# A hybrid attention and RWKV layer, its instructions ordered by the framework's timeline model

## Chip, core and metric

The kernel runs on one core of a Trainium2 chip. The metric is the device time of one execution in microseconds (us). Three runs of the kernel before gave a median of 2612.89 us (2607.87 to 2619.28).

## The reference, cut to what matters

One layer is computed for 1024 prompt tokens and for 32 decode tokens that have 256 earlier ones in a cache. All sizes are fp32; the model width is 2048, there are 8 attention heads of width 128 (two maps of 64 each) and 16 RWKV heads of 64.

```python
xn = rms_norm(x, norm_g)
proj = xn @ w_in                      # 2048 x 8320: q, k, v, gate, RWKV r/k/v, LoRA, gate
q = rope(rms_norm(q, q_norm_g), pos); k = rope(rms_norm(k, k_norm_g), pos)
o = diff_attention(q, k, v)           # (softmax of map 0 - lam * softmax of map 1) @ v, chunk mask
att_out = rms_norm(o, subln_g) * (1 - lam_init) * silu(g_att)
# RWKV-7, per token: S = S * w_t + (S a_t) b_t^T + v_t k_t^T ; y_t = S r_t
y = group_norm(wkv_scan(r, decay, k, v, -kk, kk * a, wkv0)) * lnx_g + lnx_b + bonus
rw_out = y * silu(g_rw)
out = x + concat(att_out, rw_out) @ w_out
```

## The kernel before

The tokens are worked in two halves. Half A is 512 prompt tokens and the 32 decode tokens, 544 columns in two chunks of 288 and 256; half B is the other 512 prompt tokens in one chunk. In each half there are eight units. Unit u stands for one attention head and one pair of RWKV heads and runs eight projections (q, k, v, attention gate, RWKV r, k, v and gate). A projection (`proj`) has 16 blocks of the contraction, and each fp32 product is made of three in a rounded format (`xh` by `wh`, `xl` by `wh`, `xh` by `wl`), so it is 48 matmuls for each chunk, into a PSUM bank named `pj` of which there are three. All matmuls are recorded at L92, transposes on TensorE at L97. Behind the units come 16 output projections for each half.

Weights arrive by GpSimd's DMA queue in 256 KB pieces (`wr`, two buffers; L231), are rounded by ScalarE (`wh`, L224), and the remainder is taken by VectorE (`wl`, L225; three buffers each). A finished bank is read by VectorE, which multiplies it with the row scale (`normed`, L351), and this frees the bank.

Everything else is put between the projections. RWKV of a unit is done for two sub-blocks of four or five chunks of 64 tokens: a preparation (`rw_down`: products of `AR` and `BK` in the bank `Y`, masked into `MM` at L765; a solver of 31 steps on VectorE, L784 and L786, between two trips through DRAM), then a chain (`rw_chain`) with one round per chunk of tokens. A round has three steps on TensorE in the bank `ch`, each with a handoff to other engines: `ch<-Sw,AR` (then L893 on ScalarE and `xs`, L896 on VectorE), `ch<-xs,TT` (then `UV`, L902 on ScalarE and L903 on VectorE), `ch<-UV,MM` (then the new state `Sw`, L908, and the output `Yt`, L916, on VectorE). The next round starts from the new `Sw`. Attention has the steps of q and k (norm through the bank `am`, rotation at L437 to L440, split at L446 and L462, in buffers of the tag `t`, four), the turning of v (`vT`, also a `t`; transposes in `am`), and for each of four query blocks the scores in the bank `sc`, the maximum over them (L556), exponentials, transposes of `E` in `sc`, and the product with `Vt` in `am`. PSUM is full: three banks `pj`, one each of `ch`, `am` and `Y`, two for `sc`.

The order is set twice. When the kernel is written out, its own planner does it: six streams (chain, preparation, q and k, post, attention, decay) are generators that yield a latency from the table `LAT`; between the matmuls of a projection `pump()` lets each stream go on whose due time has been passed by a clock that counts the matmuls written so far:

```python
                if k < KT - 1:
                    if k % 4 == 3 or (k % 2 == 1 and n == 512):
                        pump()
                    else:
                        chs.run()
```

Then the framework's scheduler takes the written program. It lets instructions pass engine by engine; among those that its model of time has as ready, the one with the highest priority goes, which is the one written first, or one written under `tc.high_priority()`, as the weights are. On the chip each engine runs its instructions strictly in the resulting order.

## Time and profile before

| | |
|---|---|
| median of three runs | 2612.89 us |
| the profiled execution: its time | 2613.46 us |
| its span | 2611.7 us |
| TensorE (PE) busy | 2549.7 us, 98% |
| VectorE (DVE) busy | 1892.0 us, 72% |
| ScalarE (ACT) busy | 1349.6 us, 52% |
| GpSimd (POOL) busy | 415.1 us, 16% |
| mean granted clock of TensorE | 0.995 |

The profiled execution is one run of the kernel; its times are those of the rows below. A share of busy time is a mean over the whole span. PEld is TensorE's loading of weights, which runs beside its matmuls. An fp32 matmul that isn't in the rounded format stands as two records in the trace. A matmul's duration runs to the modelled end of its pipeline, so two that follow each other overlap in the timeline. The granted clock is given as a share of 2.4 GHz; 0.50 is 1.2 GHz.

### The profile page before, as it was taken

The numbers are of one execution on the slowest core, as the hardware profiler recorded it, in microseconds if no ns is written. First come the engines' busy times: TensorE is split into PE (matmuls) and PEld (weight loads), VectorE is DVE, ScalarE is ACT, GpSimd is POOL, SyncE is SP. The second block draws the span as 40 slices with busy tenths as digits, with TensorE's granted clock in tenths as the row PEclk, the third lists the DMA queues.
The fourth block names the chain that finished last, engine by engine and source line by source line (L and its number), as shares of the span: only waits on it lengthen the run. The fifth ranks groups of instructions, "written<-read, shape, count | busy, mean of one in ns | idle before, by whom it ended". The sixth has DMA issues, their size and how long they took to land. (4 is left out here: it accounts for less than half of the span.)

```text
span 2611.7 us, 49090 instructions
## 1 busy us (share of the span) xinstructions
PE 2549.7 (98%) x17128; PEld 2220.1 (85%) x17128; DVE 1892.0 (72%) x5768; ACT 1349.6 (52%) x3138; POOL 415.1 (16%) x949
## 2 busy tenths in 40 slices
PE   7999999999999999999999999999999999999999
PEld 7999999999898999877777777777777778999887
DVE  7576877777777787788787887788878888753432
ACT  6455555555555655565555555555555556332321
POOL 3211111111111111111111111111111111111000
PEclk9999999999999999999999999999999999999999
DMA  4433332324242524353332323232324244544443
GB/s 156 119 102 94 93 103 84 110 82 115 75 122 80 170 72 122 98 153 100 98 98 87 103 83 106 85 111 81 114 81 115 77 132 118 176 148 140 137 142 108
DMA packets 198665, 286.74 MB, mean 110 GB/s; under 512 B 102097, under 2 KB 115921, under 8 KB 198417
## 3 DMA queue, kind: packets, MB, share of 16 engines
q0 software_dynamic: 51088, 169.12, 21.8%
q1 hardware_dynamic: 147328, 114.47, 15.5%
q8 instruction: 136, 2.23, 0.4%
q14 instruction: 113, 0.92, 0.1%
HBM read 228.11 MB, written 37.51 MB: 102 GB/s over the span
## 5 line engine op out<-in xcount | busy, mean ns | idle before, releaser
L92 PE MATMUL pj<-xh,wh 128*128 128x256 f32 (+2 forms) x3888 | 1294.2, 333 | 7.7 <-ACT xh L248 6.7
L92 PE MATMUL pj<-xl,wh 128*128 128x256 f32 (+2 forms) x3888 | 1274.7, 328 | 5.0 <-DVE xl L249 5.0
L92 PE MATMUL pj<-xh,wl 128*128 128x256 f32 (+2 forms) x3888 | 1272.5, 327 | 1.1 <-DVE wl L225 1.1
L92 PEld LDWEIGHTS pj<-xh,wh 128*128 128x128 f32 x3888 | 735.7, 189 | 61.2 <-ACT xh L248 7.0
L92 PEld LDWEIGHTS pj<-xl,wh 128*128 128x128 f32 x3888 | 736.2, 189 | 52.5 <-DVE xl L249 8.8
L92 PEld LDWEIGHTS pj<-xh,wl 128*128 128x128 f32 x3888 | 735.4, 189 | 52.4 <-DVE wl L225 2.1
L224 ACT CAST wh<-wr 128x512 fp32r<-128x512 f32 x584 | 360.6, 618 | 471.8 <-PE pj L92 420.1
L225 DVE TENSOR_TENSOR wl<-wr,wh 128x512 fp32r<-128x512 f32 x584 | 401.2, 688 | 193.5 <-ACT wh L224 162.9
L231 POOL DMA_DIRECT2D wr<-w_in x517 | 278.3, 538 | 1639.8 <-DVE wl L225 492.2
L786 DVE TENSOR_TENSOR ts<-tm,ts 64x54 f32<-64x54 f32 (+35 forms) x992 | 198.2, 200 | 15.1
L784 DVE TENSOR_TENSOR tm<-ts,ms 64x54 f32<-64x54 f32 (+35 forms) x992 | 197.7, 199 | 14.5 <-DMA ts<-tinit 0.2
L92 PEld LDWEIGHTS ch<-UV,MM 64*64 64x64 f32 (+2 forms) x1632 | 111.5, 145 | 38.1 <-DVE UV L903 9.2
L92 PE MATMUL ch<-UV,MM 64*64 64x64 f32 (+2 forms) x1632 | 128.9, 231 | 8.0 <-DVE UV L846 5.1
L899 ACT ACTIVATE SP<-Sw,PL 64x64 f32<-64x64 f32 x256 | 88.3, 345 | 91.2 <-DVE Sw L908 78.1
L225 DVE TENSOR_TENSOR wl<-MM,wh 128x512 fp32r<-128x512 f32 x64 | 44.0, 689 | 89.1 <-ACT wh L224 89.1
L224 ACT CAST wh<-MM 128x512 fp32r<-128x512 f32 x64 | 39.6, 620 | 128.9 <-PE pj L92 123.3
L896 DVE TENSOR_TENSOR xs<-ch,MM 64x64 f32<-64x64 f32 x272 | 58.6, 216 | 50.2 <-ACT RS L893 45.7
L908 DVE SCALAR_TENSOR_TENSOR Sw<-ch,PL,SP 64x64 f32<-64x64 f32 x256 | 70.7, 276 | 23.2 <-PE ch L92 16.7
L92 PE MATMUL am<-Vt,E 128*128 128x128 f32 (+1 forms) x592 | 84.7, 280 | 1.8 <-ACT wh L224 1.1
L92 PE MATMUL Y<-AR,BK 64*128 64x128 f32 x544 | 84.8, 290 | 0.7 <-DVE MM L765 0.6
L92 PEld LDWEIGHTS Y<-AR,BK 64*128 64x128 f32 x544 | 67.5, 188 | 19.8 <-issue 9.1
L92 PEld LDWEIGHTS am<-Vt,E 128*128 128x128 f32 (+1 forms) x592 | 73.5, 189 | 8.7 <-issue 2.6
(303 smaller groups left out, 3127.9 us busy)
## 6 DMA issues: line engine op xcount, KB each, us to landing
wr<-w_in POOLq DMA_DIRECT2D x517, 256.0 KB, 3.2
wr<-w_out POOLq DMA_DIRECT2D x64, 256.0 KB, 3.6
MM<-w_out POOLq DMA_DIRECT2D x32, 512.0 KB, 4.0
t<-xB SPq DMA_DIRECT2D x32, 256.0 KB
ms<-dm SPq DMA_DIRECT2D x96, 64.0 KB
t<-t SPq DMA_DIRECT2D x64, 68.0 KB
t<-mixd SPq DMA_DIRECT2D x16, 272.0 KB
t<-xA SPq DMA_DIRECT2D x16, 272.0 KB
```

The lines of the kernel that those rows point to most:

```text
L92: PE.matmul(out, lhsT, rhs, start=start, stop=stop)
L224: S.copy(wh, raw)
L225: V.tensor_tensor(wl, raw, wh.bitcast(F32), op=ALU.subtract)
L231: q.dma_start(raw, wsrc[:, g * 512:(g + 1) * 512].rearrange("p (k f) -> p k f", k=4))
L784: V.tensor_tensor(tm, ts_[:, 0:qn, s:s + 1].to_broadcast([R * nb, qn, m]), ms[:, s:s + 1, s + 1:32].to_broadcast([R * nb, qn, m]), op=ALU. ...
L786: V.tensor_tensor(ts_[:, 0:qn, s + 1:32], tm, ts_[:, 0:qn, s + 1:32], op=ALU.add)
L896: V.tensor_tensor(xs[64 * h:64 * h + 64], ch[low, 64 * h:64 * h + 64], MM[low, c, h, 0:64], op=ALU.add)
L899: S.activation(SP[:, h, :], S_[hr, h, :], AF.Copy, scale=PL[hr, 0, gc:gc + 1])
L908: V.scalar_tensor_tensor(S_[hr, h, :], ch[low, 192 + 64 * h:256 + 64 * h], PL[low, h, gc:gc + 1], SP[:, h, :], ALU.mult, ALU.add)
```

## The change

One argument is added where the framework's context is opened. What the kernel writes is unchanged, its planner and the table too. The scheduler, which orders the written program when it is built, now decides what is ready by another model of time, one that keeps timelines of engines, queues and DMAs.

```diff
-    with tile.TileContext(nc) as tc:
+    with tile.TileContext(nc, schedule_with_timeline_sim=True) as tc:
         build(tc, I, O)
```

No instruction is added, removed or changed by it; each engine has the same ones in another order. Numbers behind a name tell tiles of one tag apart, and xN stands for N alike in a row.

**Unit 3 (half A), TensorE.** Before, one round of the chain (bank `ch_1246`), from its first to its second step; `pj_1240` is the second bank of the RWKV r projection of unit 3:

```order
L92 MATMUL ch_1246_6781<-Sw_1245_6770,AR_1022_5589 128x128
L92 MATMUL pj_1240_6759<-xh0_19_104,wh_1242_6762 128x256
L92 MATMUL pj_1240_6759<-xl0_20_105,wh_1242_6762 128x256
L92 MATMUL pj_1240_6759<-xh0_19_104,wl_1243_6763 128x256
L92 MATMUL pj_1240_6759<-xh1_22_111,wh_1242_6762 128x256
L92 MATMUL pj_1240_6759<-xl1_23_112,wh_1242_6762 128x256
L92 MATMUL pj_1240_6759<-xh1_22_111,wl_1243_6763 128x256
L92 MATMUL pj_1240_6759<-xh2_25_118,wh_1242_6762 128x256
L92 MATMUL pj_1240_6759<-xl2_26_119,wh_1242_6762 128x256
L92 MATMUL pj_1240_6759<-xh2_25_118,wl_1243_6763 128x256
L92 MATMUL pj_1240_6759<-xh3_29_127,wh_1242_6762 128x256
L92 MATMUL ch_1246_6781<-xs_1248_6785,TT_9_79 128x64
```

Now the same round, to its third step; `Y_1143` and `Y_1157` belong to the preparation of the next sub-block, `am_1144` to the norm of q, `am_1195` to the norm of k of unit 3:

```order
L92 MATMUL ch_1246_6781<-Sw_1245_6770,AR_1022_5589 128x128
L92 MATMUL Y_1143_6231<-AR_1119_6070,BK_1109_6013 128x128 x4
L92 MATMUL am_1144_6237<-p3_1124_6100,blkr_85_252 128x272
L92 MATMUL am_1144_6237<-p3_1125_6101,blkr_85_252 128x272
L92 MATMUL ch_1246_6781<-xs_1248_6785,TT_9_79 128x64
L92 MATMUL Y_1157_6304<-AR_1119_6070,BK_1109_6013 128x128
L92 MATMUL am_1195_6460<-p3_1149_6274,blkr_85_252 128x272
L92 MATMUL am_1195_6460<-p3_1150_6275,blkr_85_252 128x272
L92 MATMUL ch_1246_6781<-UV_1108_6003,MM_1023_5597 128x64 x2
```

The projections between the steps are gone, and products of `Y` and `am` stand there; the round now comes earlier, during the projection of unit 3's attention gate. It is a part of 72 matmuls in a row with no projection among them.

**The same place, VectorE.** Now, in the middle of those 72 matmuls (L402 splits sums of squares and products in two for a sum on TensorE, L440 and L446 to q, L765 to the preparation, the others to the chain):

```order
L402 TENSOR_TENSOR p3_1150_6275<-t_1148_6270,p3_1149_6274 128x544
L402 TENSOR_TENSOR kk_1210_6549<-bo_1208_6546,p3_1209_6548 128x320
L903 COPY UV_1108_6003<-ch_1246_6781 64x64
L765 TENSOR_TENSOR MM_1120_6078<-Y_1157_6304,cst_84_250 128x2x64
L440 TENSOR_TENSOR t_1122_6095<-t_1122_6095,t_1123_6096 128x544
L908 SCALAR_TENSOR_TENSOR Sw_1245_6770<-ch_1246_6781,PL_889_4834,SP_1249_6788 64x64 x2
L916 TENSOR_TENSOR Yt_1244_6769<-ch_1246_6781,RS_1247_6783 64x128
L446 TENSOR_TENSOR Ql_7_77<-t_1122_6095,Qd_1145_6246 64x544
L765 TENSOR_TENSOR MM_1120_6078<-Y_1161_6337,cst_84_250 128x2x64
L446 TENSOR_TENSOR Ql_7_77<-t_1122_6095,Qd_1145_6246 64x544
L896 TENSOR_TENSOR xs_1263_6879<-ch_1261_6875,MM_1023_5597 64x64 x2
L903 COPY UV_1108_6003<-ch_1261_6875 64x64
```

What the chain and the preparation hand on stands here in one queue with the steps of q. Before, these lines stood among those of the solver and the weights. The end of the queue, up to the instruction (L351) that reads the bank `pj_1152` of the projection of v, was before:

```order
L784 TENSOR_TENSOR tm_1084_5884<-ts_1057_5804,ms_1056_5799 64x35
L786 TENSOR_TENSOR ts_1057_5804<-tm_1084_5884,ts_1057_5804 64x7x5
L462 TENSOR_TENSOR t_1202_6500<-t_1147_6269,Ks_1201_6499 64x544
L225 TENSOR_TENSOR wl_1222_6597<-wr_1220_6594,wh_1221_6596 128x512
L784 TENSOR_TENSOR tm_1085_5887<-ts_1057_5804,ms_1056_5799 64x28
L462 TENSOR_TENSOR t_1202_6500<-t_1147_6269,Ks_1201_6499 64x544
L786 TENSOR_TENSOR ts_1057_5804<-tm_1085_5887,ts_1057_5804 64x7x4
L225 TENSOR_TENSOR wl_1226_6643<-wr_1224_6640,wh_1225_6642 128x512
L784 TENSOR_TENSOR tm_1086_5890<-ts_1057_5804,ms_1056_5799 64x24
L351 TENSOR_TENSOR t_1212_6565<-pj_1152_6284,rb_92_272 128x288
```

and is now (L810 belongs to the preparation, `t_1147` is k):

```order
L908 SCALAR_TENSOR_TENSOR Sw_1245_6770<-ch_1261_6875,PL_889_4834,SP_1264_6882 64x64 x2
L916 TENSOR_TENSOR Yt_1244_6769<-ch_1261_6875,RS_1262_6877 64x128
L810 TENSOR_TENSOR bo_1208_6546<-Y_1218_6589,v_1003_5508 128x320
L439 TENSOR_TENSOR t_1147_6269<-t_1147_6269,t_1151_6279 128x544
L440 TENSOR_TENSOR t_1147_6269<-t_1147_6269,t_1148_6270 128x544
L896 TENSOR_TENSOR xs_1273_6948<-ch_1271_6944,MM_1023_5597 64x64 x2
L784 TENSOR_TENSOR tm_1164_6350<-ts_1163_6348,ms_1162_6343 80x31
L786 TENSOR_TENSOR ts_1163_6348<-tm_1164_6350,ts_1163_6348 80x31
L784 TENSOR_TENSOR tm_1165_6353<-ts_1163_6348,ms_1162_6343 80x30
L462 TENSOR_TENSOR t_1202_6500<-t_1147_6269,Ks_1201_6499 64x544
L351 TENSOR_TENSOR t_1212_6565<-pj_1152_6284,rb_92_272 128x288
```

L351 stands behind the same step of k (L462) in both; the solver's steps and two subtractions for weights (L225) that stood between are gone from there, and the chain's `Sw`, `Yt` and `xs` have come ahead of it.

**Unit 10 (half B), TensorE.** Before, the first two steps of a round (bank `ch_4294`):

```order
L92 MATMUL ch_4294_22050<-Sw_4167_21440,AR_4056_20925 128x128
L92 MATMUL pj_4281_21983<-xh6_2893_15716,wh_4292_22040 128x512
L92 MATMUL pj_4281_21983<-xl6_2894_15717,wh_4292_22040 128x512
L92 MATMUL pj_4281_21983<-xh6_2893_15716,wl_4293_22041 128x512
L92 MATMUL pj_4281_21983<-xh7_2896_15722,wh_4292_22040 128x512
L92 MATMUL pj_4281_21983<-xl7_2897_15723,wh_4292_22040 128x512
L92 MATMUL pj_4281_21983<-xh7_2896_15722,wl_4293_22041 128x512
L92 MATMUL pj_4281_21983<-xh8_2917_15828,wh_4303_22087 128x512
L92 MATMUL ch_4294_22050<-xs_4296_22054,TT_9_79 128x64
```

Now that round and the next (bank `ch_4311`); `sc_4373` are transposes for the attention of unit 10:

```order
L92 MATMUL ch_4294_22050<-Sw_4167_21440,AR_4056_20925 128x128
L92 MATMUL ch_4294_22050<-xs_4296_22054,TT_9_79 128x64
L92 MATMUL ch_4294_22050<-UV_4228_21728,MM_4057_20933 128x64 x2
L97 MATMUL sc_4373_22368<-cst_84_250,E0_4306_22105 128x128 x8
L92 MATMUL ch_4311_22121<-Sw_4167_21440,AR_4056_20925 128x128
L92 MATMUL ch_4311_22121<-xs_4313_22125,TT_9_79 128x64
L92 MATMUL ch_4311_22121<-UV_4228_21728,MM_4057_20933 128x64 x2
```

The seven projection matmuls between the two steps are gone, and the three steps of a round follow each other.

## Rows read from the trace of the kernel before

**Rows 1.** The page, busy time of each engine, its share of the span, instructions.

```profile
PE 2549.7 (98%) x17128; PEld 2220.1 (85%) x17128; DVE 1892.0 (72%) x5768; ACT 1349.6 (52%) x3138; POOL 415.1 (16%) x949
```

**Rows 2.** Busy time by stretch: from:to, length, each engine busy (instructions), granted clock, DMA.

```profile
0.00:65.30 65.30, 51.56 (x319) 46.84 (x320) 46.80 (x87) 44.03 (x73) 21.88 (x41) 0.92 0.49 156
...
2350.40:2415.70 65.30, 65.30 (x524) 65.30 (x524) 19.65 (x32) 13.68 (x22) 11.82 (x22) 1.00 0.46 141
...
2481.00:2546.30 65.30, 65.30 (x285) 53.09 (x284) 20.19 (x30) 14.38 (x24) 6.32 (x12) 1.00 0.45 142
2546.30:2611.60 65.30, 61.72 (x268) 49.90 (x266) 17.52 (x26) 12.41 (x20) 4.23 (x9) 1.00 0.34 108
```

**Rows 3.** TensorE's waits: engine, line, releaser: us in total, times, longest.

```profile
PE ch L92 <- DVE xs L896: 7.0, 16, 1.6
...
PE ch L92 <- DVE Yt L916: 6.1, 12, 0.8
```

**Rows 4.** The timeline, one round of the chain: start, us, engine, line, operation, tiles.

```profile
2274.44 0.38 PE L92 MATMUL ch<-Sw,AR 128*128 128x128 f32 x2
...
2274.86 0.26 ACT L893 COPY RS<-ch 64x128 f32<-64x128 f32 x1 [1.22 <-PE ch L92]
...
2275.50 0.22 DVE L896 TENSOR_TENSOR xs<-ch,MM 64x64 f32<-64x64 f32 x1
...
2275.82 0.41 PE L92 MATMUL ch<-xs,TT 128*128 128x64 f32 x2
...
2276.77 0.68 DVE L225 TENSOR_TENSOR wl<-wr,wh 128x512 fp32r<-128x512 f32 x1
...
2277.60 0.23 DVE L903 COPY UV<-ch 64x64 f32<-64x64 f32 x1
...
2277.88 0.66 PE L92 MATMUL ch<-UV,MM 128*128 128x64 f32 x4
...
2280.21 0.29 DVE L916 TENSOR_TENSOR Yt<-ch,RS 64x128 f32<-64x128 f32 x1
...
2280.65 0.46 PE L92 MATMUL ch<-Sw,AR 128*128 128x128 f32 x2
```

**Rows 5.** Groups by line and shape: form, xcount, then busy us, mean ns, idle before.

```profile
L92 PE MATMUL pj<-xh,wh 128*128 128x512 f32 x1296 | 526.4, 406 | 0.0
...
L92 PE MATMUL pj<-xh,wh 128*128 128x288 f32 x1296 | 394.6, 304 | 7.2 <-ACT xh L248 6.7 <-ACT wh L224 0.5
...
L92 PE MATMUL pj<-xh,wh 128*128 128x256 f32 x1296 | 374.4, 289 | 0.5 <-DVE t L351 0.3
...
L908 DVE SCALAR_TENSOR_TENSOR Sw<-ch,PL,SP 64x64 f32<-64x64 f32 x256 | 70.7, 276 | 23.2 <-PE ch L92 16.7
...
L765 DVE TENSOR_TENSOR MM<-Y,cst 128x512 f32<-128x512 f32 x64 | 43.7, 682 | 4.4 <-PE Y L92 3.9
...
L556 DVE TENSOR_REDUCE sm<-sc 128x1 f32<-128x1024 f32 x16 | 19.5, 1221 | 0.3
...
L440 DVE TENSOR_TENSOR t<-t,t 128x544 f32<-128x544 f32 x16 | 11.6, 724 | 2.5 <-ACT t L384 2.5
```

**Rows 6.** Busy time in single microseconds (columns as in rows 2) in mid-kernel.

```profile
842.00:843.00 1.00, 0.48 (x4) 0.29 (x3) 0.00 (x0) 0.96 (x5) 0.00 (x0) 1.00 0.00 0
843.00:844.00 1.00, 0.16 (x1) 0.19 (x2) 0.54 (x3) 0.83 (x2) 0.00 (x0) 0.94 0.46 152
844.00:845.00 1.00, 1.00 (x5) 0.88 (x6) 0.81 (x2) 0.20 (x1) 0.12 (x1) 0.50 0.85 307
...
850.00:851.00 1.00, 1.00 (x7) 1.00 (x7) 0.42 (x1) 0.64 (x2) 0.00 (x0) 0.65 0.14 37
```

**Rows 7.** TensorE's timeline over the same stretch.

```profile
841.77 0.71 PE L92 MATMUL Y<-AR,BK 64*128 64x128 f32 x4
843.84 0.62 PE L92 MATMUL ch<-xs,TT 128*128 128x64 f32 x2 [1.36 <-DVE xs L896]
844.40 1.22 PE L92 MATMUL Y<-AR,BK 64*128 64x128 f32 x4
```

## The prediction

> **What bounds the kernel now.** I read the page's busy times first, then busy time by stretch, then who waits for whom, then one piece of the timeline. TensorE is busy for 2549.7 us of the 2611.7 us span; VectorE, the next, for 1892.0 [rows 1]. TensorE stands idle for 62.0 us in all. Of that 13.7 fall in the first stretch of 65.3 us, while inputs arrive, and 3.6 in the last [rows 2]; the other 44.7 us are spread over the 35 stretches between, a little over a microsecond each. The longest entries in the list of TensorE's waits are handoffs inside the RWKV chain: 7.0 us in 16 pieces until `xs`, 6.1 us in 12 until `Yt` [rows 3]. So the kernel is bound by the work on TensorE, and the order of its instructions is good: nothing more than about 45 us can be won by any other order of the same matmuls, and the start and the end stay.
>
> What a matmul costs in that stream: where nothing but projections run, 524 records of 256 or 288 columns take 65.30 us, 0.125 us each, and 285 of 512 columns take 65.30 us, 0.229 us each [rows 2]. There are 3 x 1296 projection matmuls of each of the three widths [rows 5], so 7776 x 0.125 + 3888 x 0.229 = 1862 us. The rest of the busy time, 688 us, belongs to the 3472 other matmuls (transposes, scores, the products of `Y`, `am`, `sc` and `ch`) that the built program has: 0.20 us each.
>
> **What the change moves.** No instruction is added or removed. The program that the kernel writes is the same, and so are its priorities; only the order in which the framework lets instructions pass, engine by engine, differs. Against the order in which the kernel writes them, TensorE's 15,136 matmuls were displaced by 8 places on average; now by 59. Projections (`pj`) come 31 places earlier, `ch`, `Y`, `am` and `sc` matmuls 70 to 155 later. The queues of SyncE and GpSimd hardly move (8 and 3 places), the copies and subtractions of the weights move with the projections, and I cost the DMAs at nothing: weights were ready whenever TensorE ran projections alone (65.30 of 65.30 us busy [rows 2]). If that cover went, it would show as waits of `pj` for `wl` or `wh`.
>
> What matters is where the other matmuls went. Before, they stand in 991 groups of at most 29 between projections; now in 693 groups, of which fifteen have 26 to 84 matmuls and hold 923 of them. Six of the fifteen are in the first half (427 matmuls, one group in every second to seventh unit), six in the second (391), three around the change of halves and at the end (105). TensorE's order in units 3 and 10 above shows it: rounds of `ch`, which had 3 to 20 projections between their steps, now stand with none. TensorE passes nothing that waits, so in such a group each step pays its whole handoff. The cause stands at each group's end: the next `pj` needs a bank, and the bank is freed by a VectorE instruction (L351) that is queued behind the q and k steps (the third piece of VectorE's queue above) or the attention of the same unit.
>
> **The price of a handoff.** The timeline gives one round of the chain with projections beside it: from the first step's matmul at 2274.44 to the second's at 2275.82 1.38 us, on to the third's at 2277.88 2.06 us, on to the next round's first at 2280.65 2.77 us [rows 4]. That is 6.2 us a round, with VectorE busy with other things in between (a weight subtraction of 0.68 is in the row); by the bare durations in the same rows it is about 4.1. A round's own four matmuls keep TensorE for about 0.9 us of it (the 0.38, 0.41 and 0.66 of the rows overlap what follows). Before, projections fill the rest. To count how often it is not filled I took every matmul that waits for another engine and summed TensorE's work between it and the matmul that its producer waited for: under 1 us before in 197 places, under 0.2 in none; now in 274 and 104, and of the 274, 259 lie in the fifteen groups. Outside them there are 15 left.
>
> **The sum.** First what goes: with 15 short handoffs left outside the groups, most of the 44.7 us; I take 40.
>
> Then the groups. The 72 matmuls of the group in unit 3, of which the second piece of its order above shows a part, I walked by hand with the durations of [rows 5]: 37 rows up to the first `ch` of the rounds are 8.0 us of matmuls and 3.4 us of waits. The other 35 are 7.8 us of matmuls and 11.1 of waits: 3.2 before two first steps (VectorE has L440, 0.72, or L437 and L438 ahead of two L908, 0.28 each, and L916, 0.29), 1.3 before three second steps, 1.6 before two third steps, 3.6 before six `Y` and `am` matmuls (L765, 0.68, is what most of them wait for), 1.4 before the next projection. That is 14.5 us for 72 matmuls, 0.20 each. The same walk through the 83 matmuls in unit 10 gives 41 us for 20 us of matmuls, so 21 us of waits, 0.25 each; there VectorE also has score maxima of 1.22 us [rows 5] and the solver's steps in its queue. So 427 x 0.20 + 391 x 0.25 + 105 x 0.22 = 86 + 99 + 23 = 208 us. From below: VectorE instructions that follow one of the group's own matmuls cannot start before TensorE has got there, and these alone take 17.3 and 32.3 us in the two groups, against 15.8 and 20.3 us of matmuls; over all fifteen the excess is 79 us. From above: if the real gaps are like the 6.2 us round rather than the 4.1 us one, about 260.
>
> Then the clock. Before, TensorE's granted clock fell twice in mid-kernel, and both times behind a pause: at 842 to 844 TensorE was busy for 0.48 and 0.16 of two microseconds, and the clock was 0.50, which is 1.2 GHz, from 844 to 850.7 [rows 6]. In that time it did 40 records, which take 4.1 us at 10 a microsecond: 2.7 us lost. Two `Y` matmuls took 0.71 us before the fall and 1.22 after [rows 7], 0.72 more. In the fifteen groups TensorE would stand idle about half of the time, in pieces of up to 3 us, so I expect a fall in each. Behind each group: 15 x 2.7 = 40 us. Within: 923 x 0.20 = 185 us of matmuls, all at the lower clock 133 us more; I take 0.4 of that, 53 us, since a group begins at the full clock and part of its matmuls lie beside VectorE's work. From below 0, from above the whole 133.
>
> The Trainium skill ("TensorE: Matmul & The Clock Gate", section "Why this matters for your kernels") asks for no longer idle gaps between bursts of matmuls, or the clock drops back. Taken as a rule on single gaps, it would leave these groups, whose gaps are one to three microseconds, at 2.4 GHz, and the sum without 93 us of clock would be 2782; the trace shows a fall behind a pause of 1.36 us [rows 7], so the row decides.
>
> The profiled execution took 2613.46 us, 1.8 more than its span and 0.6 more than the median of the three shown, so I need no correction: 2613.5 - 40 + 208 + 53 + 40 = 2874.5, **2875 us**.
>
> **The rivals.**
> The clock holds: 2613.5 - 40 + 208 = 2782 us. For it: TensorE is never idle for long in one piece. Against it: [rows 6].
> The engines run side by side in the groups, so that only VectorE's excess counts: 2613.5 - 45 + 79 = 2648 us. For it: the groups mix steps of four tasks, one can fill another's wait. Against it: in unit 10 the three steps of a round follow each other with nothing between.
> The clock stays low through every group and the rounds are the long ones: 2613.5 - 30 + 260 + 133 + 40 = 3017 us.
> Faster: VectorE and ScalarE, which have slack between the groups, have done a group's work before TensorE gets there, no wait is left in them, and the 45 us are won: 2568 us. It decides from the point where VectorE's instructions in a group need none of the group's own matmuls. Against it: `xs`, `UV`, `Sw` and `MM` in the first of VectorE's queues above read `ch` and `Y` of the same group.
> No change: the order differs only where it does not matter, 2613 us. Against it: over 10,000 lines of difference on TensorE, and the floor of 79 us of which 45 at most come back.
>
> **How the numbers follow.** Chances: 0.56 for the forecast, 0.24 for a clock that holds, 0.11 for engines side by side, 0.04 for the long case, 0.03 faster, 0.02 no change. Half a per cent, 13 us, is about what a measurement of this kernel can tell from no change. So slower 0.95, within it 0.02, faster 0.03. For a range that leaves out no more than 2 in 10 I take 2700, below the rival with the full clock and its waits a third less, to 2990, near the long case: it holds nearly all of the first two cases.
>
> **What would show it.** Right: TensorE's idle time grows from 62 to some 250 us, in fifteen stretches of 30 to 50 us, in which it is half idle and VectorE nearly full, with projections at 0.125 and 0.229 us between them; the list of waits is led by `ch` for `UV`, `Yt` and `xs` and `Y` for `MM`; waits outside the groups are below 20 us; the row of granted clocks shows 7 or 8 where it shows 9. The step on the clock is wrong if the clock stays at 1.00 in the stretches, the step on handoffs if a group of 72 matmuls takes under 20 us. The whole is wrong if TensorE's idle time falls below 62 us, or if projections wait for weights.

## The result

The changed kernel takes 2845.72 us (median of four runs, 2842.62 to 2847.34), the kernel before 2611.03 (also of four): a ratio of 1.088 (95% interval 1.086 to 1.090), or 235 us more. Forecast were 2875 us, 261 more. The profiled execution took 2847.34 us with a span of 2845.6.

The busy time of the engines and the row of granted clocks in 40 slices, from the page of the changed kernel (compare [rows 1]):

```profile
PE 2649.2 (93%) x17128; PEld 2348.1 (83%) x17128; DVE 1940.7 (68%) x5768; ACT 1346.5 (47%) x3138; POOL 403.7 (14%) x949
...
PEclk9998989798989798989989898979898998899999
```

The same 17,128 records keep TensorE busy for 2649.2 us instead of 2549.7, 99.5 more, and it stands idle for 196.4 us instead of 62.0, 134.4 more. Both together are the whole difference. The row of clocks, which had a 9 in each slice, now has a 7 or an 8 in 16 of them.

The fifteen groups are there, as fifteen stretches. Busy time in five of them and the sum over all fifteen (columns as in [rows 2]; the five are those of units 3, 5, 6 and 10 and the last of all):

```profile
495.40:527.50 32.10, 23.07 (x123) 18.38 (x123) 17.93 (x47) 14.60 (x42) 1.80 (x8) 0.58 0.26 72
...
801.10:824.40 23.30, 19.44 (x116) 15.59 (x115) 16.71 (x40) 13.76 (x37) 1.17 (x7) 0.56 0.28 82
946.10:987.50 41.40, 29.14 (x140) 22.03 (x139) 23.39 (x64) 27.41 (x72) 1.37 (x8) 0.56 0.42 129
...
1869.60:1913.10 43.50, 27.57 (x136) 21.81 (x134) 32.31 (x122) 16.76 (x47) 0.85 (x3) 0.61 0.19 50
...
2420.20:2438.10 17.90, 9.93 (x52) 7.89 (x50) 11.33 (x36) 8.03 (x22) 0.31 (x2) 0.65 0.32 76
sum 442.90, PE 294.05 PEld 227.29 DVE 299.84 ACT 204.56 POOL 17.11; mean PE 19.60 PEld 15.15 DVE 19.99 ACT 13.64 POOL 1.14
```

All fifteen last 442.9 us, in which TensorE is busy for 294.05 and idle for 148.9; the granted clock in them is 0.56 to 0.67. VectorE is busy for 68% of them. TensorE's longest entries among its waits (compare [rows 3]):

```profile
PE ch L92 <- DVE xs L896: 28.3, 23, 2.3
PE ch L92 <- DVE UV L846: 22.4, 11, 4.3
PE ch L92 <- DVE UV L903: 20.8, 27, 3.8
PE ch L92 <- DVE Yt L916: 16.9, 16, 2.0
...
PE pj L92 <- DVE t L351: 6.3, 9, 1.3
```

The chain's handoffs lead, as forecast, with `xs` at 28.3 us instead of 7.0; only the second line, `UV` of L846, is no handoff within a round (it is taken up below). The last line stands for nine waits of a projection for the bank that L351 had to read. Three of them stand at the end of one of the fifteen stretches (371.4, 671.1 and 1138.2 us), a fourth end waits 0.9 us for another L351, and at the other eleven ends the projection waits for nothing over 0.15 us.

Two rounds show the two halves. In unit 3 (first half), TensorE's timeline over one round, from the first step to the next round's first:

```profile
509.50 0.63 PE L92 MATMUL ch<-Sw,AR 128*128 128x128 f32 x2
510.06 2.07 PE L92 MATMUL Y<-AR,BK 64*128 64x128 f32 x8
512.06 0.82 PE L92 MATMUL am<-p,blkr 128*128 128x272 f32 x2
512.68 0.52 PE L92 MATMUL ch<-xs,TT 128*128 128x64 f32 x2
513.13 0.79 PE L92 MATMUL Y<-AR,BK 64*128 64x128 f32 x2
513.85 0.82 PE L92 MATMUL am<-p,blkr 128*128 128x272 f32 x2
514.59 1.11 PE L92 MATMUL ch<-UV,MM 128*128 128x64 f32 x4
...
516.97 0.65 PE L92 MATMUL ch<-Sw,AR 128*128 128x128 f32 x2
```

No wait stands in it at all. The round takes 7.5 us because everything in it runs at 1.2 GHz: four products of `Y` as eight records take 2.07 us. In unit 10 (second half) the three steps have nothing between them:

```profile
1879.22 0.63 PE L92 MATMUL ch<-Sw,AR 128*128 128x128 f32 x2
1881.99 0.66 PE L92 MATMUL ch<-xs,TT 128*128 128x64 f32 x2 [2.14 <-DVE xs L896]
1883.78 1.12 PE L92 MATMUL ch<-UV,MM 128*128 128x64 f32 x4 [1.13 <-DVE UV L903]
...
1887.20 0.63 PE L92 MATMUL ch<-Sw,AR 128*128 128x128 f32 x2
```

Here 2.14 and 1.13 us of waits stand in brackets, and the round takes 8.0 us.

### The profile page after: what moved, and what is told of

Same layout as the page of the kernel before. It is cut to its first block, busy times and chain, and to the rows that moved or that the text cites. A ratio compares the mean times of both kernels' runs of the same rounds, so it can differ in the third digit from the quotient of the medians.

```text
span 2845.6 us, 49125 instructions
## 1 busy us (share of the span) xinstructions
PE 2649.2 (93%) x17128; PEld 2348.1 (83%) x17128; DVE 1940.7 (68%) x5768; ACT 1346.5 (47%) x3138; POOL 403.7 (14%) x949
## 4 chain that ended last, share of the span: by engine, by line
PE 74%; DVE 9%; DMA 7%; issue 4%; ACT 3%; SPq 2%; POOL 0%; DVEq 0%; POOLq 0%; ACTq 0%
PE pj L92 56%; PE ch L92 6%; PE Y L92 3%; PE am L92 3%; PE sc L92 2%; SPq L174 2%; DMA wr<-w_in 2%; DVE wl L225 1%; DMA k<-dt 1%; PE sc L97 1%; DVE ts L786 1%; DVE tm L784 1%; DMA dt<-ts 1%; PE am L97 1%; DMA ms<-dm 1%
## 5 line engine op out<-in xcount | busy, mean ns | idle before, releaser
L92 PE MATMUL pj<-xh,wh 128*128 128x288 f32 (+2 forms) x3888 | 1286.4, 332 | 15.8 <-ACT xh L248 6.7
L92 PEld LDWEIGHTS pj<-xh,wh 128*128 128x128 f32 x3888 | 746.7, 192 | 74.0 <-DVE t L351 7.7
L92 PEld LDWEIGHTS pj<-xl,wh 128*128 128x128 f32 x3888 | 747.9, 192 | 61.2 <-DVE xl L249 9.3
L92 PEld LDWEIGHTS pj<-xh,wl 128*128 128x128 f32 x3888 | 744.2, 192 | 57.0 <-DVE wl L225 2.3
L224 ACT CAST wh<-wr 128x512 fp32r<-128x512 f32 x584 | 360.9, 618 | 500.6 <-PE pj L92 363.8
L225 DVE TENSOR_TENSOR wl<-wr,wh 128x512 fp32r<-128x512 f32 x584 | 400.9, 687 | 214.1 <-ACT wh L224 200.7
L784 DVE TENSOR_TENSOR tm<-ts,ms 64x54 f32<-64x54 f32 (+35 forms) x992 | 200.1, 202 | 65.2 <-DMA ms<-dm 40.8
L92 PE MATMUL ch<-UV,MM 64*64 64x64 f32 (+2 forms) x1632 | 149.0, 252 | 57.8 <-DVE UV L846 22.4
L92 PEld LDWEIGHTS ch<-UV,MM 64*64 64x64 f32 (+2 forms) x1632 | 132.3, 165 | 84.8 <-DVE UV L903 27.5
L92 PE MATMUL Y<-AR,BK 64*128 64x128 f32 x544 | 105.1, 336 | 3.7 <-ACT os L509 2.1
L225 DVE TENSOR_TENSOR wl<-MM,wh 128x512 fp32r<-128x512 f32 x64 | 44.0, 689 | 90.2 <-ACT wh L224 90.2
L224 ACT CAST wh<-MM 128x512 fp32r<-128x512 f32 x64 | 39.6, 620 | 130.6 <-PE pj L92 126.1
L92 PEld LDWEIGHTS Y<-AR,BK 64*128 64x128 f32 x544 | 84.0, 227 | 20.2 <-issue 7.7
L92 PEld LDWEIGHTS am<-Vt,E 128*128 128x128 f32 (+1 forms) x592 | 81.9, 211 | 13.8 <-DVE bo L948 7.2
L92 PEld LDWEIGHTS ch<-xs,TT 128*128 128x128 f32 x272 | 50.6, 216 | 39.6 <-ACT RS L893 19.1
```

The costliest lines, as they stand in the source:

```text
L92: PE.matmul(out, lhsT, rhs, start=start, stop=stop)
L224: S.copy(wh, raw)
L225: V.tensor_tensor(wl, raw, wh.bitcast(F32), op=ALU.subtract)
L784: V.tensor_tensor(tm, ts_[:, 0:qn, s:s + 1].to_broadcast([R * nb, qn, m]), ms[:, s:s + 1, s + 1:32].to_broadcast([R * nb, qn, m]), op=ALU. ...
```

## The experiments

Most of them chain an engine's instructions in an order taken from one of the two kernels. The chain sets only the order of issue and adds no wait for an end; the engines that are not chained are ordered by the framework around it.

```diff
+def pin(tc, orders):
...
+    dep = mybir.DependencyInfo(mybir.DependencyClass.NoSync, mybir.DependencyReason.DATA)
+    for eng, text in orders.items():
...
+        row = [mine[k] for k in perm]
+        for x, y in zip(row, row[1:]):
+            tc.add_manual_dep(y, x.name, dep, reason="order")
...
     with tile.TileContext(nc) as tc:
         build(tc, I, O)
+        pin(tc, ORDERS)
```

Here `mine` are the engine's instructions as the kernel writes them and `perm` the wanted order.

**The measure: everything chained as in the changed kernel.**

> All five engines chained in the order of the changed kernel, nothing else altered: the measure for the three runs with that chaining (zero matmuls, round trips, fixed weights). If chaining itself moves nothing: 2840 to 2852 us, as the changed kernel. If it moves something, that part has to be taken out of the three.

2838.36 us, ratio 1.0865 (1.0846 to 1.0884), just under the expected 2840 to 2852. The interval overlaps with that of the changed kernel (1.086 to 1.090), so chaining moves nothing that can be told. The runs below that chain all five engines are held against this one.

**TensorE's order alone, put in and taken back.** The first has the old scheduler and `ORDERS` for TensorE from the changed kernel, the second the new scheduler and `ORDERS` for TensorE from the kernel before.

> The scheduler of before, but TensorE's 15,136 matmuls are chained in the order that they have in the changed kernel; the other four engines are ordered by the model of before around that. My theory (TensorE's order alone makes the time: fifteen groups of 26 to 84 matmuls without projections, handoffs in order, and the clock): 2790 to 2870 us, fifteen stretches at the lower clock, some 190 us of TensorE idle. Rival (the new order of VectorE's, ScalarE's and the DMA queues makes it, and TensorE only waits for them): 2611 to 2700 us.

> The changed kernel, but TensorE's matmuls are chained in the order that they have in the kernel before; the other engines are ordered by the timeline model around that. My theory: 2600 to 2640 us, TensorE idle 50 to 80 us, no group, the clock at 1.00 nearly throughout. Rival (other engines' order): over 2700 us.

With the new order on TensorE alone 3019.42 us, ratio 1.157 (1.154 to 1.160); with the old order on TensorE alone 2785.81, ratio 1.067 (1.064 to 1.070). My theory failed in both. The first lies outside of both cases: TensorE's new order is worse still when the other engines are ordered by the old model around it. Its waits in that kernel:

```profile
PE ch L92 <- DVE UV L846: 83.0, 14, 10.0
...
PE pj L92 <- DVE t L351: 21.8, 11, 5.3
```

The second went the rival's way: there is no group left, and yet some 177 us of the loss stay. Where VectorE waits for DMAs in that kernel, under it in the changed kernel, and last in the kernel before:

```profile
DVE UV L846 <- DMA k<-dt: 83.0, 27, 5.3
...
DVE tm L784 <- DMA ms<-dm: 28.2, 16, 4.2
```

```profile
DVE tm L784 <- DMA ms<-dm: 40.8, 24, 4.6
DVE UV L846 <- DMA k<-dt: 38.6, 15, 6.7
```

```profile
DVE UV L846 <- DMA k<-dt: 4.9, 7, 1.0
```

In the kernel before L784 never waits for `ms`. L784 opens the solver and L846 the chain, each behind a trip through DRAM. VectorE comes to them before the data, and passes nothing while it stands.

Neither of the two runs exchanges one engine's order and keeps the others, though. By the names in the traces, VectorE in the second has another instruction than the changed kernel at 4938 of its 5768 places, and another than the kernel before at 4226: the scheduler gave it a third order. What TensorE's old order would be worth among the changed kernel's other four is not shown.

**Two engines held to the written order.** Both have the changed kernel's scheduler:

```diff
     with tile.TileContext(nc, schedule_with_timeline_sim=True) as tc:
-        build(tc, I, O)
+        with tc.manual_schedule(engines={mybir.EngineType.Activation}):
+            build(tc, I, O)
```

> The changed kernel with one thing more: ScalarE keeps the order in which the kernel writes its instructions; all other engines are ordered by the timeline model. In the built program the fifteen groups are gone (one of 26 matmuls is the largest) and there are 660 groups of other matmuls between projections, where before has 991. My theory (the groups make the loss, not the model): 2560 to 2650 us; in the traces of before and after, a matmul behind one of the other kind (projection or not) keeps TensorE some 0.07 to 0.10 us longer than one behind its own kind, so 331 groups less may be worth up to 53 us. Rival (the timeline model's order is bad elsewhere too): over 2700 us.

> The changed kernel with VectorE kept in the order in which the kernel writes its instructions. In the built program eight groups of 28 to 30 matmuls are left (232 matmuls instead of 923), 666 groups in all. My theory: 232 matmuls at 0.16 us of waits and 0.14 us of clock each are 70 us, less up to 52 us for 325 groups less: 2600 to 2690 us. Rival (VectorE's queue is what TensorE waits for, so an unhelpful order of VectorE costs more): over 2700 us.

3551.81 us (1.361, 1.358 to 1.365) and, with `DVE` for `Activation`, 4607.23 us (1.765, 1.760 to 1.770). Both lie far beyond my theory, in the rivals' case (over 2700), and the thought behind the theory fell with it, that a TensorE without groups must be fast. TensorE's first wait in the one and in the other:

```profile
PE pj L92 <- ACT wh L224: 137.3, 104, 17.8
```

```profile
PE pj L92 <- DVE wl L225: 559.0, 157, 21.1
```

Weights come late here: L224 and L225 have a high priority, by which both models put them ahead of their written place, and an engine that is held to the written order can't. As measures of the groups the two runs are void; they show what an engine's order is worth that doesn't fit the others.

**The old orders put back one engine after the other**, in the changed kernel:

> The changed kernel with TensorE and VectorE both chained in the order of the kernel before; ScalarE and the queues are ordered by the timeline model around that. With TensorE's order alone taken back 2786 us were measured, with VectorE waiting 83.0 us in front of L846 and 28.2 in front of L784 for DMAs. If VectorE's order makes those 177 us over before: 2605 to 2640 us. If ScalarE's or the queues' order has a part in it: over 2680 us.

> The changed kernel with TensorE, VectorE and ScalarE chained in the order of the kernel before; only the queues of SyncE and GpSimd are ordered by the timeline model. With the first two taken back 2739 us were measured, with ScalarE waiting 87.3 us for weights in front of L224. If ScalarE's order makes those 129 us over before: 2600 to 2635 us. If the DMA queues' order has a part in it: over 2680 us.

> The changed kernel with VectorE alone chained in the order of the kernel before. The model then makes 654 groups on TensorE (991 before, 693 in the changed kernel), eight of them with 27 to 35 matmuls, 240 in all, and none larger. If VectorE's order is what the model gets wrong, and the groups follow from it: 2570 to 2680 us. If TensorE's order is bad with any order of VectorE: over 2750 us.

| taken from the kernel before | time, us | ratio to before (95%) |
|---|---|---|
| nothing (the changed kernel) | 2845.72 | 1.088 (1.086 to 1.090) |
| TensorE | 2785.81 | 1.067 (1.064 to 1.070) |
| TensorE, VectorE | 2738.99 | 1.050 (1.048 to 1.052) |
| TensorE, VectorE, ScalarE | 2652.83 | 1.017 (1.015 to 1.019) |
| VectorE alone | 3325.09 | 1.273 (1.270 to 1.276) |

Each step of the first four rows gives something back: 60, 47 and 86 us, and the last 43 are left to the queues of SyncE and GpSimd (by elimination: no run puts their old order back too; by the names in the traces SyncE's has another transfer than the kernel before at 176 of 1104 places). I had put the rest of the loss on one engine each time: the second step went the rival's way, and the third ended between the two cases. VectorE alone makes it worse (the case over 2750); ScalarE then waits for weights:

```profile
ACT wh L224 <- DMA wr<-w_in: 668.2, 349, 5.6
```

In the kernel before this is 32.9 us. The steps can't be added up as shares of the engines: another sequence would give other ones, and in each run the engines that are left free get an order that neither kernel has, by the names in the traces. What the runs show is that no one or two engines' old order brings the old time back while the timeline model orders the rest.

**The round trips through DRAM taken out of VectorE's way**, with all five engines chained as in the changed kernel:

```diff
+        flatin = I["tinit4" if cn == 4 else "tinit5"].rearrange("p f -> (p f)")
...
-            dma(ms[w * nb:(w + 1) * nb], dm.rearrange("b g s t -> (b g) s t"))
+            dma(ms[w * nb:(w + 1) * nb], flatin.rearrange("(b s t) -> b s t", s=32, t=32))
...
+        src = I["tinit4" if cn == 4 else "tinit5"].rearrange("p f -> (p f)").rearrange(
+            "(b g s t) -> b g s t", b=2, s=32, t=32)
-        dtg = dt.rearrange("b (c h) s t -> b h s c t", h=2)
+        dtg = src.rearrange("b (c h) s t -> b h s c t", h=2)
...
-            dma(t01[32 * b:32 * b + 32], dt[b, :, 0:32, :].rearrange("g s t -> s g t"))
+            dma(t01[32 * b:32 * b + 32], src[b, :, 0:32, :].rearrange("g s t -> s g t"))
```

> All five engines are chained in the order of the changed kernel. The loads of `ms` (for the solver) and of `TT` and `k2` (for the chain) read a constant of the same size instead of the DRAM pieces dm and dt, which are still written but read by nobody, so the output is another: VectorE no longer waits for the two round trips through DRAM (in the changed kernel 40.8 us in front of L784 and 38.6 us in front of L846). If those waits cost next to nothing because the handoffs of the groups would last as long anyway (the prediction, which had no such term): 2830 to 2850 us. If they are a part of the loss, since VectorE passes nothing while it waits: 2740 to 2800 us. If they are its main cause: below 2700 us.

2809.74 us, ratio 1.077 (1.075 to 1.078): 29 us less than the measure. VectorE's two waits have not gone, since the loads stand where they stood in the queue, but they are less than half. In the measure, and under it in this kernel:

```profile
DVE tm L784 <- DMA ms<-dm: 46.0, 24, 4.9
...
DVE UV L846 <- DMA k<-dt: 33.2, 15, 6.7
```

```profile
DVE tm L785 <- DMA ms<-tinit: 20.2, 13, 3.9
...
DVE UV L849 <- DMA k<-tinit: 12.8, 12, 3.6
```

So these waits are a part of the loss, and some 46 us of them less gave 29 us. The time lies between two of the expected ranges, closer to that of this case (2740 to 2800).

**The weights taken out of ScalarE's way**, chained in the same manner:

```diff
+    fixed = []
...
+        if fixed:
+            raw = fixed[0].unsqueeze(1).to_broadcast([128, 4, 128])
         S.copy(wh, raw)
         V.tensor_tensor(wl, raw, wh.bitcast(F32), op=ALU.subtract)
...
+    fixed.append(ident)
```

> All five engines are chained in the order of the changed kernel. The rounding of the weights (L224 and L225) reads a constant that lies in SBUF instead of the piece that was loaded, so the output is another; the loads of the weights are still issued, but nobody waits for them. In the changed kernel ScalarE waited 96.3 + 8.2 us in front of L224 for weights (32.9 + 9.8 before). If that is a part of the loss, since the chain's copies stand behind L224 in ScalarE's queue: 2770 to 2815 us. If it is hidden, as the prediction had it, which cost the loads at nothing: 2835 to 2850 us.

2852.85 us, ratio 1.094 (1.092 to 1.097): no gain, 14 us more than the measure and just over the range of the hidden case. ScalarE's waits in front of the rounding for pieces of `w_in`, 105.3 us in the measure's trace, are 2.3 us in this one, and no time came back for it: the prediction was right to cost these at nothing. Where the 14 us come from is not shown; VectorE's waits for `ms` are 54.5 us against 46.0.

**TensorE kept busy in seven of the groups**, chained as before:

```diff
+    def fill(out, rhs):
+        for _ in range(FILL.get(nth[0], 0)):
+            PE.matmul(out, zero, rhs, start=False, stop=False)
+        nth[0] += 1
...
         PE.matmul(out, lhsT, rhs, start=start, stop=stop)
+        fill(out, rhs)
```

> All five engines are chained in the order of the changed kernel. Added are 365 matmuls of 128 x 128 by 256 or 288 columns with zeros as weights, which add nothing to the projection that is under way: they stand at 52 places of seven of the fifteen groups (the six of the first half and the last), each ahead of a matmul that waited there for 0.2 us or more, sized to 0.9 of that wait; 52 us of waits in all. In these seven groups 165 us passed at the lower clock. If the clock falls because TensorE pauses (my theory), it stays up there, and by rows 7 (0.71 us at the full clock, 1.22 at the lower) about 0.42 of 165 us comes back: 2760 to 2800 us, although work is added. If the clock follows something else: 2845 to 2880 us.

2811.61 us, ratio 1.077 (1.074 to 1.080): 27 us less than the measure, with 365 matmuls more, between the two expected ranges. Four of the fifteen stretches and the sum of all, in this kernel:

```profile
489.30:517.10 27.80, 26.20 (x183) 22.55 (x183) 17.63 (x45) 14.36 (x41) 2.22 (x8) 0.82 0.28 80
...
788.00:810.60 22.60, 20.92 (x144) 17.55 (x143) 16.43 (x39) 13.77 (x37) 1.18 (x7) 0.77 0.29 86
...
1839.10:1883.10 44.00, 26.81 (x135) 21.19 (x134) 32.27 (x121) 16.74 (x47) 0.85 (x3) 0.63 0.17 49
...
2390.40:2406.50 16.10, 14.24 (x107) 12.07 (x105) 10.90 (x35) 8.49 (x24) 0.00 (x1) 1.00 0.34 86
sum 430.40, PE 323.33 PEld 263.11 DVE 297.02 ACT 201.51 POOL 16.80; mean PE 21.56 PEld 17.54 DVE 19.80 ACT 13.43 POOL 1.12
```

The stretch of unit 3 is the first line: 27.8 us at a clock of 0.82, which was 32.1 at 0.58; the second had 0.56 and now 0.77; the last had 0.65 and now 1.00. The third line is one of the eight without fillers, as slow as before. So the clock does follow from what TensorE does in the groups, and work that does nothing buys time. In the whole kernel TensorE is busy for 2659.4 us, only 9.6 more than in the measure in spite of the added matmuls, and idle for 41 us less.

The clock came back by less than expected. By the lengths and clocks of the seven stretches, 81 us in them still pass at 1.2 GHz, of the 165; the one that gained least went from 29.8 us at 0.59 to 29.9 at 0.66. The seven together are 12.8 us shorter (198.5 to 185.7), so more than half of the gain lies outside of them: with mean clocks of 0.920 and 0.941, and less what the fifteen stretches hold, the time at 1.2 GHz elsewhere falls from some 100 to some 60 us. The fillers were sized to 47 us of work (0.9 of 52), TensorE is now busy for 26.2 of 27.8 us in the first line, and how short the groups would be at the full clock without them is not shown.

**Fewer changes between projections and other matmuls**, in the kernel before:

```diff
                     if k % 4 == 3 or (k % 2 == 1 and n == 512):
                         pump()
-                    else:
-                        chs.run()
```

> The kernel before with one line of its planner taken out: between the matmuls of a projection the chain is no longer let on at every block, only where all streams are. In the built program TensorE then changes 864 times from projections to other matmuls, where before has 991. In before a matmul behind one of the other kind keeps TensorE about 0.16 us longer for a change there and back. If that is a price of the change itself: 127 x 0.16 = 20 us less, 2580 to 2602 us. If it is only the way in which the trace divides the time, or if the later steps cost waits: 2605 to 2640 us.

2608.06 us, ratio 0.9989 (0.9976 to 1.0002, twelve runs): no difference that can be told, the second of the expected cases. The first line of its page and the one of busy times:

```profile
span 2600.3 us, 49026 instructions
...
PE 2522.9 (97%) x17128; PEld 2218.0 (85%) x17128; DVE 1886.2 (73%) x5768; ACT 1339.0 (51%) x3138; POOL 412.9 (16%) x949
```

TensorE is busy for 26.8 us less (2549.7 before), 0.21 us for each of the 127 changes that went, and idle for 77.4 us, 15 more. So TensorE's busy time does follow the number of changes. That fewer changes save time is not shown: these two executions (the fastest of twelve here, one above the median before) differ by 11 us, the medians by less than 3.

## Why the prediction was right, and where it wasn't

The time, the side and the place came out. Term by term, against the profiled execution before:

| term | forecast, us | measured, us |
|---|---|---|
| waits outside the groups | -40 | -14.5 (62.0 to 196.4 - 148.9 = 47.5) |
| waits in the groups | +208 | +148.9 |
| the clock, inside the groups | +53 | +130 (longer matmuls; some 107 of it the clock) |
| the clock, behind the groups | +40 | +31 (all outside the groups) |
| fewer changes between kinds of matmuls | none | -62 (the remainder) |
| sum | +261 | +233 |

The measured column: the 923 matmuls of the groups, followed record by record through both traces, keep TensorE busy for 294 us now and for 164 before, hence 130. By the ratio in [rows 7] (0.71 to 1.22 us) some 107 of it are the clock, since some 254 of the 294 us passed at 1.2 GHz; the rest is not told apart. Behind the groups: a mean clock of 0.92 over 2845.6 us is 455 us at half the clock, the fifteen stretches hold 355 of it by their own clocks, and 26 us were there before; of the 74 left 0.42 are 31. Only some 58 us at 1.2 GHz lie right behind a stretch, the rest in falls elsewhere, so the term as it was forecast is 24. (The 2.7 us of the forecast come from 40 records counted once in each microsecond that they touch; the trace has 28 of them. The rate of 10 is counted the same way, so the 2.7 stand.) The last term is what remains of the 99.5 us of busy time, 99.5 - 130 - 31, and it agrees with the 0.21 us of the experiment on changes: 298 changes less (991 to 693 groups) would be 63 us by it. That is an estimate; no run takes this term by itself.

**What goes elsewhere** was mis-sized. I had counted short handoffs in the order and put all waits down to them. Record by record, 16 of the 62 us stood at matmuls that are now in the groups; the other waits, some 46 us with start and end, did not shrink (47.5).

**The handoffs in the groups** were taken too long, and **the clock within them** too short, and I read the two errors as one. I walked the groups at the full clock and then added the clock. But a matmul at half the clock fills time that would have been a wait: the round of unit 3 above has no wait and still takes 7.5 us. In half B, where the steps stand alone, the waits come closer: 76 us in six groups, forecast 99 (unit 10's has 15.9, forecast 21), against 46 of 86 in half A. So waits and clock should not be added up. No run holds the clock up in a group without adding work to it, so this reading is argued from the traces. That the sum came out within 28 us is luck in good part: measured less forecast, its terms are off by +25, -59, +77, -9 and -62.

**What starts the groups** has a part that I had not seen. The cause that the prediction names, a projection that waits for L351, shows at four of the fifteen ends only. I costed the DMAs at nothing because weights were ready, and looked only at weights. The long group of unit 3 opens with this (microseconds 495 to 502, columns as in [rows 6], then the timeline of the same place):

```profile
495.00:496.00 1.00, 1.00 (x8) 0.79 (x8) 0.54 (x2) 0.94 (x2) 0.00 (x0) 1.00 0.10 16
...
497.00:498.00 1.00, 0.00 (x0) 0.00 (x0) 0.00 (x0) 0.00 (x0) 0.00 (x0) 1.00 0.57 84
498.00:499.00 1.00, 0.00 (x0) 0.00 (x0) 0.00 (x0) 0.00 (x0) 0.00 (x0) 1.00 0.74 229
499.00:500.00 1.00, 0.00 (x0) 0.00 (x0) 0.00 (x0) 0.00 (x0) 0.00 (x0) 1.00 1.07 329
...
501.00:502.00 1.00, 0.58 (x11) 0.45 (x9) 0.97 (x4) 0.36 (x1) 0.11 (x1) 0.50 0.00 0
```

```profile
496.60 0.93 SPq L174 DMA_DIRECT2D k<-dt  x2
...
500.04 0.43 DVE L846 STREAM_TRANSPOSE UV<-k 32x256 f32<-32x256 f32 x1 [4.50 <-DMA k<-dt]
...
500.52 0.69 PE L92 MATMUL ch<-UV,MM 32*32 32x32 f32 x9 [4.28 <-DVE UV L846]
```

For three microseconds TensorE, VectorE and ScalarE all stand at 0.00. VectorE is in front of L846, whose load `k<-dt` was issued at 496.60 and is read at 500.04; TensorE waits 4.28 us for it, and when it goes on the clock is at 0.50. In the kernel before VectorE came to L846 when the data lay there (4.9 us in all against 38.6). Of TensorE's 22.4 us until L846, 19.6 stand behind such a wait of VectorE: 14.2 in seven of the stretches, and 5.3 outside of all, in places where the forecast had no wait. So the handoffs proper are less than the 148.9 us in the table, some 135.

**That TensorE's order alone makes the time** was the theory that I took into the experiments, and it fell. In the changed kernel's trace the loss does lie in the groups, but the old order of TensorE does not bring the time back when the timeline model orders the rest, and the new one with the old model's neighbours costs 174 us more than the change itself. So the place of the loss is read from the traces; what two runs took out of it are 27 us (the clock in seven groups) and 29 us (the two DMA waits), and no run takes the groups away and leaves the rest as it is. The prediction had said that the queues hardly move and that only VectorE's queue matters at the groups' ends; 43 us of the loss were left when only the DMA queues were still ordered by the new model.

**The rivals.** A clock that holds (2782) did not: it is 0.56 to 0.67 in every stretch. Engines side by side (2648) needed VectorE to be the limit there; it is busy for 68%. The long case, faster and no change did not come.

**The signs that I named.** Right: fifteen stretches, the lower clock in them, projections at their old pace between (a matmul of 512 columns by `xh` and `wh` takes 404 ns, 406 before), the chain at the head of the waits. Wrong: 196 us of idle time instead of some 250, stretches of 18 to 44 us instead of 30 to 50, in which TensorE is idle for a third of the time instead of half, a VectorE that is far from full, and 28 us of waits outside the groups besides start and end (15.7 and 3.7), where I had said under 20. `Y` for `MM` is not among the leading waits.

## What to carry to other kernels

Engines that run strictly in order need orders that fit each other: VectorE's order from the fast schedule, with the rest ordered around it by the other model, made a kernel slower than either (3325 us). When a scheduler's model is exchanged, look first for runs of dependent steps on the bounding engine with nothing independent between, and for instructions on any engine that now stand in front of data that has yet to land. A sum over such a run has to be walked at the clock that will be granted there, since slow matmuls can hide waits, and waits added to a slow clock then count the same time twice.

## What was not expected of the hardware

The clock needed no long pause to fall. In the stretch from 801.1 to 824.4 TensorE is busy for 19.44 of 23.3 us and the granted clock is 0.56; its longest waits there, and the two microseconds at which the clock falls, are

```profile
PE ch L92 <- ACT TT L858: 0.7, 1, 0.7
PE Y L92 <- ACT MM L800: 0.7, 1, 0.7
PE am L92 <- PE ch L92: 0.5, 1, 0.5
```

```profile
803.00:804.00 1.00, 0.48 (x12) 0.40 (x9) 0.68 (x4) 0.49 (x2) 0.00 (x0) 1.00 0.07 26
804.00:805.00 1.00, 1.00 (x17) 0.69 (x15) 0.14 (x1) 0.81 (x2) 0.00 (x0) 0.56 0.70 252
```

The Trainium skill ("TensorE: Matmul & The Clock Gate", section "Why this matters for your kernels") asks for no long idle gaps between bursts of matmuls, and taken as a rule on single gaps it would have kept this stretch at 2.4 GHz. The trace disagrees, and decides: small matmuls with waits of 0.5 us and less stood before the fall here, those of 0.7 us behind it, and zeros multiplied in the waits brought the clock from 0.56 to 0.77.

The second is that TensorE's busy time falls with the number of changes between the projections' matmuls and the others, by 0.21 us for each there and back (26.8 us for 127), which nothing in the list of waits shows, since TensorE counts as busy. How much of it is time that a kernel can win is open, since the run with 127 changes less was no faster.
